# Moving the scans' first copies out of PSUM to ScalarE, and some products to other banks

## The chip, the cores and the metric

The kernel runs on one core of a Trainium2 chip. TensorE multiplies matrices and writes to PSUM, which has eight banks of 512 f32 values in each of 128 partitions; VectorE and ScalarE read PSUM and work on SBUF; GpSimd works on SBUF alone; the queues of SyncE and ScalarE issue DMAs here. The profile calls them PE (with PEld for its weight loads), DVE, ACT, POOL and SP. The metric is the device time of one run in microseconds (us), lower is better.

## The reference

A trunk of two residual layers on 512 tokens of width 1024: a spatial-gating MLP, a gated convolutional FFN, an RWKV-7 time mixing, a second FFN, and a final RMS norm, all in float32. The change lies in the time mixing, whose core for each of 16 heads of width 64 is

```python
def step(state, inp):
    r_t, w_t, k_t, v_t, a_t, b_t = inp
    sa = jnp.einsum('bhvk,bhk->bhv', state, a_t)
    state = (state * w_t[:, :, None, :]
             + sa[..., None] * b_t[:, :, None, :]
             + v_t[..., None] * k_t[:, :, None, :])
    y_t = jnp.einsum('bhvk,bhk->bhv', state, r_t)
    return state, y_t
...
bonus = jnp.sum(r_h * k_h * r_k.astype(f32), -1, keepdims=True) * v_h
y = (y + bonus.reshape(B, S, D)).astype(h.dtype)
return (y * g) @ w_o
```

with y normalized for each head before the bonus is added.

## The kernel before

Activations lie transposed: features on the 128 partitions, the 512 tokens along the free dimension, eight tiles of two heads each (a "pair"). A dense product is made of three matmuls of rounded high and low parts (lines 325 to 327, `mm3`).

The recurrence is done in chunks of 64 tokens (`NCH` = 8). For each pair, `products` (lines 970 to 988) makes the triangular matrices of all chunks, and `invert(g)` inverts them for a head group g of four pairs: a long chain of small VectorE steps (lines 1042 to 1061), then block products on TensorE (lines 1081 and 1084) with copies on ScalarE (lines 1089, 1094, 1096). `scan(g)` then goes through the eight chunks of a group in order, twice (g = 0 and 1). A chunk has three steps, with a `yield` after each:

1. TensorE makes the first products of the four pairs into the first half of a bank `us` (line 1292); VectorE copies them to `wt` in SBUF (line 1295); TensorE adds the old state's part to the output bank `e` (line 1296); GpSimd scales the state (line 1301).
2. TensorE multiplies `wt` by the inverse into the second half of `us` (line 1305): the solutions, for head 0 of each pair in partitions 0 to 63, for head 1 in 64 to 127. VectorE copies the first half of the partitions into `vu` (line 1306), ScalarE the second (line 1307).
3. TensorE makes the new state's part from `vu` (line 1312), VectorE adds it to the scaled state (line 1316, two instructions), which the next chunk's line 1292 reads; TensorE finishes the outputs in `e` (line 1317), and ScalarE copies them to `y` (line 1320).

After every second chunk, `finish` normalizes the outputs: a square (line 1333), a sum (line 1338), a scaling (line 1348), a transpose on TensorE into "aux" (line 1354), and the combination with the bonus (line 1357).

`weave` runs other work between these steps, at rates written out by hand: `fill` is a chain of `projections` (keys and values, dense products into banks "mm"), `gates` and `project` (the output projection, into "mm"); `gate_mix` makes operands (lines 1105, 1106, 237, 238). For each value, `value(m, v)` makes two products more: four centring matmuls (line 865) into a bank that ScalarE copies out in four parts (line 870), and, once the pair m is in the set `done`, the bonus product (line 880), which VectorE multiplies by v (line 882). `done` has all `KT` = 8 pairs when `pairs` has ended, a little before `scan(0)`.

PSUM has four tags, "mm", "aux", "e" and "us", with two banks each; a tile that asks for a bank waits until one of its tag is free. The first product of `scan` uses one bank of "us" and one of "e" in each chunk.

The order of the instructions on each engine is planned when the program is built: a planner with its own estimates of durations gives an engine the instruction traced earliest of those that it takes to be ready. `issue_after` puts instructions behind a given one on its engine; `step` does so for each step of `finish`, behind the last instructions traced on TensorE and VectorE. Two engines that touch the same bank are made to wait for each other. At run time each engine keeps the planned order.

Of the kernel before, what the change touches and what calls it, by code (L numbers as in the profile page):

```python
# [22 lines left out]
KT = 8  # L23
# [121 lines left out]
class Emit:  # L145
# [622 lines left out]
    def rwkv_main(self, r, ctx, gain):  # L768
        nc, tc, A = self.nc, self.tc, self.A
        V, S, G = nc.vector, nc.scalar, nc.gpsimd  # L770
        h0, h1 = slice(0, 64), slice(64, 128)
        H = (h0, h1)
# [6 lines left out]
        def tile_(shape, tag, bufs):  # L779
            return ep.tile(shape, F32, tag=tag, bufs=bufs, name=self.uid(tag))  # L780
# [7 lines left out]
        def bc(t, n):  # L788
            return t.unsqueeze(2).to_broadcast([t.shape[0], t.shape[1], n])

        ks, used, done, vdone = {}, set(), set(), set()
        l2 = []

        ti = [ip.tile([P, 4, NCH, C], F32, name=f"ti{g}") for g in range(2)]
# [13 lines left out]
        def projections():  # L808
# [29 lines left out]
            for m in range(KT):  # L838
                a = self.acc("mm")
                w = load.take()  # L840
                if m == KT - 2:
                    ga["w"] = load_gate(0)
                for n, _ in enumerate(self.dense_steps(a, w, xv)):
                    yield
                    next(late, None)
                    if m == KT - 1 and n == 0:
                        gw[0] = gate_weights(ga["w"])
                        ga["parts"] = self.gate_parts()
                    if m == KT - 1 and len(gx) < 2:
                        gx.append(gate_mix(len(gx)))  # L850
                for _ in late:
                    yield
                v = ip.tile([P, T], F32, tag="v", bufs=1, name=self.uid("v"))
                S.copy(v, a)
                late = value(m, v)
# [3 lines left out]
        def value(m, v):  # L859
            g, i = divmod(m, 4)  # L860

            vt = ip.tile([P, NCH, C], F32, tag="vt", bufs=1, name=self.uid("vt"))
            q = self.acc("mm")
            for b in range(4):
                nc.tensor.matmul(q[:, b * P:(b + 1) * P], v[:, b * P:(b + 1) * P], self.c("center", P),
                                 start=True, stop=True)
            q4 = q.rearrange("p (b h f) -> p b h f", b=4, h=2)
            for hd in range(2):
                for par in range(2):
                    S.copy(vt[H[1 - hd], par::2, :], q4[H[par], :, hd, :])  # L870
            nc.sync.dma_start(vtd[:, :, m].rearrange("c p f -> p c f"), vt)
            yield
            yield

            while m not in done:
                yield
            wb = ip.tile([P, P], F32, tag="wb", bufs=1, name=self.uid("wb"))
            S.activation(wb, self.c("bones", P), AF.Copy, scale=self.p("r_k", m))
            q = self.acc("mm")
            nc.tensor.matmul(q, wb, rt[g][:, i, :], start=True, stop=True)  # L880
            b = rt[g][:, i, :]
            V.tensor_tensor(b, q, v, ALU.mult)  # L882
            S.activation(b, b, AF.Identity, bias=self.p("ln_b", m))
            vdone.add(m)
            yield
# [372 lines left out]
        def scan(g, late=iter(())):  # L1258

            ih = [(i, hd) for i in range(4) for hd in (1, 0)]  # L1260
            y = None

            def batch(one, lead=None):

                for n, (i, hd) in enumerate(ih):
                    with ExitStack() as behind:
                        if lead is not None:
                            behind.enter_context(tc.issue_after(lead))
                        one(i, hd, n)
                    if lead is None:  # L1270
                        lead = self.last(mybir.EngineType.PE)
                return lead

            for c in range(NCH):
                last = c == NCH - 1
                if (g, c) not in chunks:
                    load(g, c)
                st, bt, vu = chunks.pop((g, c))
                if (g, c) != (1, NCH - 1):
                    load(g + last, (c + 1) % NCH)  # L1280
                if c % 2 == 0:
                    y = tile_([P, 4, 2, C], "y", 3)
                us = self.acc("us").rearrange("p (a i f) -> p a i f", a=2, i=4)
                e = self.acc("e")
                spare[:] = [e[:, 256:]]
                e = e.rearrange("p (a i f) -> p a i f", a=2, i=4)

                def both(i, hd, n):
                    o = C + P * hd + n * C
                    return st[i][:, o:o + C]  # L1290

                lead = batch(lambda i, hd, n: nc.tensor.matmul(us[H[hd], 0, i, :], both(i, hd, 0), vu[:, hd, i, :],
                                                               start=True, stop=True))
                wt = tile_([P, 4, C], "wt", 4)
                V.tensor_copy(wt, us[:, 0])
                batch(lambda i, hd, n: nc.tensor.matmul(e[H[hd], 0, i, :], st[i][H[hd], 0:C], vu[H[hd], hd, i, :],
                                                        start=i == 0, stop=False, skip_group_check=True), lead)
                if not last:
                    s0 = tile_([P, 4, C], "wt", 4)
                    for hd in range(2):  # L1300
                        G.tensor_tensor(s0[H[hd]], vu[H[hd], hd], bc(gc[H[hd], 4 * g:4 * g + 4, c], C), ALU.mult)
                self.step(late)
                yield
                for i, hd in ih:
                    nc.tensor.matmul(us[H[hd], 1, i, :], ti[g][H[hd], i, c, :], wt[H[hd], i, :], start=True, stop=True)  # L1305
                V.tensor_copy(vu[h0, 0], us[h0, 1])
                S.copy(vu[h1, 1], us[h1, 1])
                self.step(late)
                yield
                lead = None  # L1310
                if not last:
                    lead = batch(lambda i, hd, n: nc.tensor.matmul(us[H[hd], 0, i, :], bt[:, i, hd, :], vu[:, hd, i, :],
                                                                   start=True, stop=True))
                    nvu = chunks[g, c + 1][2]
                    for hd in range(2):
                        V.tensor_tensor(nvu[H[hd], hd], us[H[hd], 0], s0[H[hd]], ALU.add)
                batch(lambda i, hd, n: nc.tensor.matmul(e[H[hd], 0, i, :], both(i, hd, 1), vu[:, hd, i, :],
                                                        start=False, stop=True, skip_group_check=True), lead)
                for hd in range(2):
                    S.copy(y[H[c % 2], :, hd, :], e[H[hd], 0])  # L1320
                self.step(late)
                yield
                if c % 2 == 1:
                    yield from late
                    late = finish(g, c // 2, y)
            left.append(late)
# [102 lines left out]
        for _ in range(LEAD):  # L1429
            next(fill, None)  # L1430
        self.weave(scan(0), inv, fill, *RATES[2], ktiles=STEPS[2])
        for _ in inv:
            pass
        self.weave(scan(1, left.pop()), None, fill, *RATES[3], ktiles=STEPS[3])
        rest, left = left.pop(), None
        next(rest)
# [79 lines left out]
```

## Time and profile before

| | before |
|---|---|
| median of 3 runs (lowest to highest) | 1250.29 us (1249.78 to 1250.6) |
| the profiled execution | 1250.9 us |
| its span | 1248.8 us |
| granted TensorE clock | 0.999 |

The profile has one row for each instruction of one execution. A row of a group tells the line, engine, operation, output and inputs with their shapes and the count, then busy time, the mean ns of one, and the idle time of the engine before them with what ended it. A row of the timeline has the start and length in us first, and in brackets the idle time before it with its releaser. Matmuls overlap, so two starts are closer together than the length of one.

### The profile page before, as it was taken

Reading aid. Unit: us, or ns where it says so; the run is one execution under the profiler, and the core shown is the slowest. Engines: PE = TensorE matmul, PEld = TensorE weight load, DVE = VectorE, ACT = ScalarE, POOL = GpSimd, SP = SyncE. Lnnn points to the kernel's source line nnn. Section 1 sums busy time; section 2 is a strip of 40 time slices with the busy share of each in tenths; the row PEclk is TensorE's granted clock in tenths of the full one; section 3 lists DMA queues with packets and bytes.
Section 4 is the critical chain, followed back from the end, with each engine's and each line's share of the span. In section 5 each row is a group of like instructions: output and inputs, shape, how many; then the busy total and the mean of one; then the engine's idle time right before and its main releaser. Section 6 shows DMA issues by size and latency. Waiting matters only on the chain. (4 is left out here: it accounts for less than half of the span.)

```text
span 1248.8 us, 19409 instructions
## 1 busy us (share of the span) xinstructions
PE 1230.6 (99%) x7535; PEld 998.3 (80%) x7535; DVE 852.0 (68%) x1418; ACT 631.5 (51%) x1089; POOL 83.0 (7%) x106
## 2 busy tenths in 40 slices
PE   9999999999999999999999999999999999999997
PEld 7878888888888888877777777778888888888886
DVE  5566568888986444774989698766777777772323
ACT  6544445555554433475777657433544444442322
POOL 1100200000000010000000012322000000000000
PEclk9999999999999999999999999999999999999999
DMA  8232457877656776326878788654232233233332
GB/s 274 92 109 80 132 170 233 249 243 243 215 171 201 228 221 193 95 92 182 228 203 240 210 259 237 221 170 128 92 101 92 94 101 102 89 93 98 105 93 81
DMA packets 125132, 201.65 MB, mean 161 GB/s; under 512 B 39856, under 2 KB 63152, under 8 KB 125040
## 3 DMA queue, kind: packets, MB, share of 16 engines
q10 hardware_dynamic: 38976, 112.87, 29.6%
q1 hardware_dynamic: 86064, 87.54, 22.7%
q8 instruction: 59, 0.97, 0.3%
q14 instruction: 33, 0.27, 0.1%
HBM read 152.93 MB, written 47.45 MB: 160 GB/s over the span
## 5 line engine op out<-in xcount | busy, mean ns | idle before, releaser
L237 ACT CAST w<-w 128x512 fp32r<-128x512 f32 x340 | 205.9, 611 | 344.2 <-PE aux L327 89.1
L238 DVE TENSOR_TENSOR w<-w,w 128x512 fp32r<-128x512 f32 x340 | 230.2, 679 | 180.3 <-ACT w L237 179.8
L325 PE MATMUL mm<-mxh,w 128*128 128x512 f32 x408 | 168.2, 412 | 2.1 <-DVE rt L882 1.6
L327 PE MATMUL mm<-mxh,w 128*128 128x512 f32 x408 | 160.2, 393 | 0.0
L326 PE MATMUL mm<-mxl,w 128*128 128x512 f32 x408 | 160.0, 392 | 0.0
L325 PEld LDWEIGHTS mm<-mxh,w 128*128 128x128 f32 x408 | 76.7, 188 | 23.8 <-issue 4.4
L327 PEld LDWEIGHTS mm<-mxh,w 128*128 128x128 f32 x408 | 76.6, 188 | 16.6 <-issue 0.4
L326 PEld LDWEIGHTS mm<-mxl,w 128*128 128x128 f32 x408 | 76.7, 188 | 15.8 <-issue 1.7
L575 ACT ACTIVATE cv<-z,par 128x512 f32<-128x512 f32 x88 | 71.7, 817 | 34.9 <-DVE z L573 30.1
L325 PE MATMUL aux<-mxh,w 128*128 128x512 f32 x216 | 84.5, 391 | 0.0
L325 PE MATMUL us<-mxh,w 128*128 128x512 f32 x216 | 84.5, 391 | 0.0
L327 PE MATMUL aux<-mxh,w 128*128 128x512 f32 x216 | 84.2, 390 | 0.0
L326 PE MATMUL us<-mxl,w 128*128 128x512 f32 x216 | 84.1, 389 | 0.0
L326 PE MATMUL aux<-mxl,w 128*128 128x512 f32 x216 | 84.1, 389 | 0.0
L327 PE MATMUL us<-mxh,w 128*128 128x512 f32 x216 | 84.1, 389 | 0.0
L354 POOL TENSOR_TENSOR ss<-ss,sq 128x512 f32<-128x512 f32 x24 | 31.8, 1327 | 761.0 <-ACT sq L352 761.0
L325 PE MATMUL e<-mxh,w 128*128 128x512 f32 x208 | 81.4, 392 | 0.0
L326 PE MATMUL e<-mxl,w 128*128 128x512 f32 x208 | 81.2, 390 | 0.0
L327 PE MATMUL e<-mxh,w 128*128 128x512 f32 x208 | 81.0, 389 | 0.0
L576 DVE SCALAR_TENSOR_TENSOR cv<-z,par,cv 128x512 f32<-128x512 f32 x88 | 66.0, 751 | 19.4 <-ACT cv L575 19.4
L577 DVE SCALAR_TENSOR_TENSOR cv<-z,par,cv 128x512 f32<-128x512 f32 x88 | 66.0, 752 | 2.9
L238 DVE TENSOR_TENSOR pwl<-pw,pwh 128x512 fp32r<-128x512 f32 (+1 forms) x51 | 34.8, 682 | 21.1 <-DMA wod<-pwl 7.2
(1107 smaller groups left out, 2564.6 us busy)
## 6 DMA issues: line engine op xcount, KB each, us to landing
w<-in_wup ACTq DMA_DIRECT2D x88, 512.0 KB, 3.7
w<-in_wdn ACTq DMA_DIRECT2D x32, 512.0 KB, 3.6
st<-std SPq DMA_DIRECT2D x15, 640.0 KB, 6.3
w<-wkd ACTq DMA_DIRECT2D x16, 512.0 KB, 5.0
w<-wvd ACTq DMA_DIRECT2D x16, 512.0 KB, 4.9
w<-wod ACTq DMA_DIRECT2D x16, 512.0 KB, 4.4
w<-in_wdn ACTq DMA_DIRECT2D x16, 384.0 KB, 3.5
w<-in_wsu ACTq DMA_DIRECT2D x8, 512.0 KB, 3.7
```

What stands on the lines that cost most here:

```text
L237: nc.scalar.copy(hi[r, :n], src)
L238: (lo_eng or nc.vector).tensor_tensor(lo[r, :n], src, hi[r, :n].bitcast(F32), ALU.subtract)
L325: mm(acc, wh, xh, start=first, stop=False)
L326: mm(acc, wh, xl, start=False, stop=False)
L327: mm(acc, wl, xh, start=False, stop=last)
L354: nc.gpsimd.tensor_tensor(self.ss, self.ss, self.sq, ALU.add)
L575: nc.scalar.activation(c, z[:, 2:], AF.Identity, scale=cw(2, i), bias=self.p("conv_b", l * 44 + i))
L576: nc.vector.scalar_tensor_tensor(c, z[:, 1:T + 1], cw(1, i), c, ALU.mult, ALU.add)
L577: nc.vector.scalar_tensor_tensor(c, z[:, 0:T], cw(0, i), c, ALU.mult, ALU.add)
```

## The change

```diff
         def value(m, v):
             g, i = divmod(m, 4)
 
+            def bank():
+                return self.acc("mm" if len(done) < KT else "aux")
+
             vt = ip.tile([P, NCH, C], F32, tag="vt", bufs=1, name=self.uid("vt"))
-            q = self.acc("mm")
+            q = bank()
...
             S.activation(wb, self.c("bones", P), AF.Copy, scale=self.p("r_k", m))
-            q = self.acc("mm")
+            q = bank()
...
-                us = self.acc("us").rearrange("p (a i f) -> p a i f", a=2, i=4)
+                us, ux = (self.acc("us").rearrange("p (a i f) -> p a i f", a=2, i=4) for _ in range(2))
...
-                V.tensor_copy(wt, us[:, 0])
+                S.copy(wt, us[:, 0])
...
                 for i, hd in ih:
-                    nc.tensor.matmul(us[H[hd], 1, i, :], ti[g][H[hd], i, c, :], wt[H[hd], i, :], start=True, stop=True)
+                    nc.tensor.matmul((us, ux)[hd][H[hd], 1, i, :], ti[g][H[hd], i, c, :], wt[H[hd], i, :], start=True, stop=True)
                 V.tensor_copy(vu[h0, 0], us[h0, 1])
-                S.copy(vu[h1, 1], us[h1, 1])
+                S.copy(vu[h1, 1], ux[h1, 1])
```

In each chunk of both scans the copy of the first products (line 1295) is made by ScalarE. The solutions of head 1 go into a second bank of "us", `ux`, from which ScalarE copies them. In `value`, both products are put into a bank of "aux" in place of "mm" when they are traced after all pairs are done.

## The prediction

> **What bounds the kernel now.** I read the first part of the page, then the windows of the two scans, then the waits, and last the timeline at single places.
>
> ```profile
> span 1248.8 us, 19409 instructions
> ...
> PE 1230.6 (99%) x7535; PEld 998.3 (80%) x7535; DVE 852.0 (68%) x1418; ACT 631.5 (51%) x1089; POOL 83.0 (7%) x106
> ```
>
> TensorE is the bound: it is busy for all but 18 us of the span. A change that takes no matmul away can win only idle time of TensorE. All of this change lies in the two scans and the work woven into them, from 719 us (the last products of `products`) to 846 us. The next rows are windows of that part: length, then busy time of PE, PEld, DVE, ACT and POOL (with counts), clock, DMA share, GB/s.
>
> ```profile
> 719.00:728.50 9.50, 8.12 (x132) 5.88 (x130) 8.88 (x26) 7.13 (x16) 1.25 (x2) 1.00 0.59 162
> 728.50:767.60 39.10, 36.69 (x520) 27.12 (x519) 36.96 (x89) 22.41 (x49) 10.38 (x12) 1.00 0.94 286
> 767.60:788.50 20.90, 19.32 (x461) 15.27 (x460) 14.77 (x31) 16.65 (x28) 6.48 (x9) 1.00 0.70 214
> 788.50:846.00 57.50, 56.77 (x780) 43.30 (x780) 39.67 (x87) 20.36 (x47) 15.62 (x16) 1.00 0.55 181
> ```
>
> TensorE is idle for 1.4 + 2.4 + 1.6 + 0.7 = 6.1 us of these 127 us. That is the ceiling, about 0.5% of the kernel. From 728.5 to 767.6 VectorE is nearly full as well (36.96 of 39.10 us, with the inversion for the second head group), while ScalarE works 22.41 us. From 767.6 to 788.5 it is the other way about: ScalarE 16.65 of 20.90, VectorE 14.77. So VectorE has too much to do in the first stretch and ScalarE in the second.
>
> What ended TensorE's idle time from 719 to 846 us (total, times, longest):
>
> ```profile
> PE us L1305 <- DVE wt L1295: 2.2, 3, 0.9
> PE mm L325 <- DVE rt L882: 1.6, 2, 1.4
> PE us L1292 <- PE e L1317: 0.6, 1, 0.6
> PE e L1317 <- issue: 0.4, 1, 0.4
> PE aux L1354 <- DVE y L1348: 0.4, 1, 0.4
> PE us L1312 <- ACT vu L1307: 0.3, 1, 0.3
> PE mm L880 <- ACT vt L870: 0.3, 1, 0.3
> PE aux L1081 <- ACT off L1094: 0.2, 1, 0.2
> ```
>
> Together 6.0 us, which agrees with the windows. Four rows belong to the three edits: the wait for the copy L1295, the waits for a bank of "mm" that the values hold (readers L882 and L870), and the wait for L1307. They add up to 2.2 + 1.6 + 0.3 + 0.3 = 4.4 us. The places of the four longest:
>
> ```profile
> 727.00 0.50 PE L325 MATMUL mm<-mxh,w 128*128 128x512 f32 x1 [1.38 <-DVE rt L882]
> ...
> 730.95 0.68 PE L1305 MATMUL us<-wt,ti 64*64 64x64 f32 x16 [0.65 <-DVE wt L1295]
> ...
> 759.50 0.68 PE L1305 MATMUL us<-wt,ti 64*64 64x64 f32 x16 [0.65 <-DVE wt L1295]
> ...
> 786.17 0.68 PE L1305 MATMUL us<-wt,ti 64*64 64x64 f32 x16 [0.94 <-DVE wt L1295]
> ```
>
> **The change part by part.** *Values in "aux".* At 727.00 a new accumulator of a projection finds no bank: one of the two of "mm" is full, the other holds the bonus product until L882 has read it, and L882 stands in VectorE's queue among the inversion's steps. As I read the loops, that product (the fifth value's) is traced in the steps behind the last pairs, when all are done, so it moves to "aux", as do both products of the last three values; no instruction is added. This takes away 1.6 us and, where the second product of the last value waits for the copies of the first (L870), 0.3 us: 1.9 us. In "aux" the values meet the transposes L1354 and the inversion's products, with two banks for all. Each holds its bank for its readers only, as it does now; I put a new wait there at nothing, and at most at the 1.9 us that the same products cost in "mm".
>
> *The copy on ScalarE.* Durations (mean ns behind the bar's busy time), VectorE first, then ScalarE:
>
> ```profile
> L1295 DVE COPY wt<-us 128x256 f32<-128x256 f32 x16 | 6.8, 423 | 1.1 <-PE us L1292 0.8
> ...
> L1306 DVE COPY vu<-us 64x256 f32<-64x256 f32 x15 | 6.2, 413 | 8.4 <-PE us L1305 8.4
> ```
>
> ```profile
> L1307 ACT COPY vu<-us 64x256 f32<-64x256 f32 x15 | 5.5, 367 | 27.4 <-DVE vu L1306 24.1 <-issue 3.1
> ...
> L1204 ACT CAST mxh<-rt 128x256 fp32r<-128x256 f32 x4 | 1.4, 402 | 0.5 <-DVE rt L1200 0.5
> ```
>
> Sixteen copies of 0.42 us (6.8 us) leave VectorE. A ScalarE copy of 128x256 out of PSUM is not in the trace: the same number of columns out of PSUM takes 0.37 us (L1307), a cast of the same shape 0.40 us. I take 0.37 us; the difference would be 0.5 us of ScalarE time over 16 chunks, which nothing waits for. What counts is not these 0.05 us but the queue: at 730.95, 759.50 and 786.17 the copy stood behind other work of VectorE. If ScalarE is free when L1292 ends, all 2.2 us go. Behind the copy on ScalarE stand casts of the gates, copies of values and inversion, and the issue of weight loads:
>
> ```profile
> w<-wod ACTq DMA_DIRECT2D x16, 512.0 KB, 4.4
> ```
>
> The copy waits for a group of 16 matmuls (0.68 us in the rows of L1305), so a load can be issued that much later; the loads are ordered a weight ahead, and I cost this at nothing (at most 0.7 us, once, if a weight comes late).
>
> The Trainium skill (page "ScalarE: Activation LUTs", Rules for kernel authors) speaks against this edit: simple arithmetic belongs on VectorE, which it puts at up to about three times as fast per element in bf16. The rows here are f32 out of PSUM and show ScalarE slightly ahead, 367 against 413 ns for the same 64x256 shape. By the rule taken at its word a copy would last up to 1.3 us, 16 times, and the 2.2 us would turn into a loss; by the rows they do not, and I go by the rows.
>
> *The halves of the solutions in two banks.* L1307 follows L1306 every time, because the program makes two engines on one bank wait for each other (24.1 us of ScalarE's idle time ends there). Apart, L1307 can start with L1306, and the solutions are complete about 0.4 us earlier in each chunk. Elsewhere dense matmuls cover that; the one place where TensorE waits for L1307 gives 0.3 us. A chunk now takes both banks of "us", so the next chunk's L1292 finds one only when L1307 or L1316 has read it. It needs L1316's result anyway: nothing.
>
> *What keeps the sum from 4.4 us.* Of it, 1.9 + (2.2 - 0.9) = 3.2 us lie before 767.6, where VectorE is almost full. L1306 and L1316 stay on VectorE in a fixed order among the inversion's steps, so TensorE cannot run further ahead than VectorE does:
>
> ```profile
> 734.40 0.67 DVE L1042 STREAM_TRANSPOSE li<-li 128x256 f32<-128x256 f32 x1
> ...
> 734.96 0.37 DVE L1316 TENSOR_TENSOR vu<-us,wt 64x256 f32<-64x256 f32 x1
> ```
>
> Here, at the end of the first chunk, L1316 follows an inversion step without idle time, and the next chunk's L1292 waits for it. What VectorE gains is five copies of 0.42 us (chunks 0 to 4), 2.1 us, and at most its 39.10 - 36.96 = 2.1 us of idle time. So the 3.2 us become between 2.1 (idle time of no use) and 3.2. I take 2.2, near the lower end, since the row shows VectorE without slack at the place that decides. What is late next is then L1316. From 767.6 on the 0.9 and the 0.3 us remain; against them I set 0.2 us for copies queued on the fuller ScalarE (bounds in the last rival). Sum: 2.2 + 0.9 + 0.3 - 0.2 = **3.2 us**. After 846 us TensorE has work throughout, so this reaches the end.
>
> **The base.** The profiled run took 1250.9 us, 2.1 us more than its span of 1248.8 and 0.6 us above the median of 1250.29. 1250.9 - 3.2 = 1247.7 in that run, and the median becomes **1247.1 us**.
>
> **The rivals.** *The whole of it.* If the order planned at build time puts L1306 and L1316 ahead of inversion steps, nothing caps the gain: 4.4 us, and with all other waits 6.0 us at most: 1245.9, at the lowest 1244.3. For it: the order is planned anew. Against: the inversion's steps are traced earlier, so the planner prefers them.
>
> *VectorE's order takes it back.* TensorE reaches L1312 and L1292 earlier and waits there for L1306 and L1316. Then of the 3.2 us only one copy's time or so is kept early on, and what is saved later is half lost to ScalarE: 0.4 + 1.2 / 2 = 1.0 us, 1249.3. For it: VectorE is 94.5% busy there. Against: the inversion's end is not awaited for long, so its steps can slip.
>
> *The fifth value stays in "mm".* If its bonus product is traced one step before the last pair is counted as done, the bank is chosen as now and the 1.6 us stay. 0.3 + 1.3 us are left before 767.6, which VectorE can follow: 1.6 + 0.9 + 0.3 - 0.2 = 2.6 us at best, and some 2.2 with the cap, 1248.1. For it: the product follows close behind the last pairs' matmuls. Against: it comes with the last steps of the first inversion, which the program walks through after the pairs.
>
> *Slower: the copy gets stuck in ScalarE's queue.* It decides where an instruction that is itself waiting is planned ahead of the copy.
>
> ```profile
> 737.97 0.68 PE L1305 MATMUL us<-wt,ti 64*64 64x64 f32 x16
> ...
> 738.95 0.62 ACT L237 CAST mxh<-sq 128x512 fp32r<-128x512 f32 x1 [2.57 <-DVE sq L1106]
> ...
> 769.37 1.04 ACT L1089 COPY ti<-li 32x1024 f32<-32x1024 f32 x1
> ...
> 769.51 0.39 PE L1305 MATMUL us<-wt,ti 64*64 64x64 f32 x6
> ```
>
> Behind the cast L237 the copy would end at 738.95 + 0.62 + 0.37 = 739.94, 2.0 us after L1305 starts today. Behind the inversion's copy L1089 it would end at 770.78, 1.3 us late. Two of each are 6.6 us; the 2.2 us for the copy are then not won, the other 2.2 are: 1250.3 + 6.6 - 2.2 = 1254.7. It turns the sign beyond some 2.2 us of such waits, so from two of them on. Against it: at most chunks ScalarE is idle when L1292 ends. The Trainium skill (page "Perfetto Trace Analysis", Per-engine timelines) has ScalarE and VectorE as strict FIFO; L1307's rows, which wait while later work stands behind, agree.
>
> **How the numbers follow.** Forecast 0.40, the whole of it 0.15, taken back 0.23, fifth value unmoved 0.10, slower 0.12. A measurement of this kernel tells about 0.2%, 2.5 us, from no change. Faster by more: nearly all of the forecast (0.36), the first rival and a part of the third (0.04), 0.55; within: the rest of the forecast (0.04), of the third (0.06) and the second, 0.33; slower: 0.12, by the last. The range goes from 1244.3 (every wait gone) to 1251.0 (the second rival and the smallest cases of the last).
>
> **What would show it.** In the changed profile L1295's group is on ScalarE at about 370 ns, x16; the 24.1 us before L1307 are gone; the waits of L325 for L882 and of L1305 for VectorE are gone; TensorE's idle time from 719 to the scans' end falls from 6.0 to some 2.8 us, and a wait of L1292 or L1312 for L1316 or L1306 appears. The inversion's steps end about 2 us earlier. I am wrong if L1305 waits for ScalarE by more than 1 us in all, if the values wait in "aux", or if TensorE's idle time moves to another place of the scans.

## The result and the profile after

The changed kernel takes 1248.05 us (median of 19 runs, 1247.38 to 1250.88), the kernel before, in 19 runs beside it, 1250.39 us. The ratio is 0.9981, with a 95% interval from 0.9975 to 0.9987: 2.3 us less, where 3.2 were forecast. The profiled execution took 1249.26 us. Its page:

```profile
span 1247.5 us, 19410 instructions
...
PE 1230.1 (99%) x7535; PEld 998.0 (80%) x7535; DVE 846.3 (68%) x1402; ACT 638.1 (51%) x1105; POOL 81.9 (7%) x106
```

Sixteen instructions have left VectorE (1418 to 1402) and come to ScalarE (1089 to 1105). TensorE does the same work. The windows of the scans again; columns as before:

```profile
719.00:728.50 9.50, 9.50 (x166) 7.48 (x166) 8.86 (x27) 7.12 (x15) 0.42 (x1) 1.00 0.54 150
728.50:767.60 39.10, 35.78 (x516) 26.38 (x514) 35.78 (x85) 24.41 (x55) 10.90 (x15) 1.00 0.92 287
767.60:788.50 20.90, 20.48 (x491) 16.43 (x487) 14.13 (x29) 18.39 (x34) 6.43 (x8) 1.00 0.70 225
788.50:846.00 57.50, 56.62 (x753) 43.10 (x752) 36.33 (x78) 23.59 (x54) 15.19 (x16) 1.00 0.57 185
```

TensorE's idle time is now 0 + 3.3 + 0.4 + 0.9 = 4.6 us, against 6.1. It has gone from the first window, fallen from 1.6 to 0.4 us in the third, and *grown* in the second, from 2.4 to 3.3 us. What ended it (total, times, longest):

```profile
PE us L1315 <- DVE rb L1309: 1.4, 1, 1.4
PE us L1295 <- issue: 1.0, 2, 0.8
PE mm L1129 <- ACT mxh L237: 0.8, 1, 0.8
PE us L1315 <- DVE vu L1309: 0.7, 1, 0.7
PE us L1308 <- ACT wt L1298: 0.2, 1, 0.2
PE aux L868 <- ACT v L854: 0.2, 1, 0.2
```

The lines of the scan have numbers higher by 3 than before, so L1315 is the old L1312 (the new state), L1309 the old L1306 (VectorE's copy of the solutions), L1295 the old L1292 (the first products) and L1298 the copy that moved. The waits for a bank of "mm" are gone, and the waits of 2.2 us for the copy have become one of 0.2. In their place stand two waits for L1309, 2.1 us, that were not there. The moved copy and its neighbour on ScalarE, by groups, and what ended their idle time:

```profile
L1298 ACT COPY wt<-us 128x256 f32<-128x256 f32 x16 | 6.0, 373 | 9.1 <-PE us L1295 8.8
...
L1310 ACT COPY vu<-us 64x256 f32<-64x256 f32 x15 | 5.5, 367 | 17.4 <-PE us L1308 14.4 <-DMA st<-std 2.0 <-issue 0.9
```

A copy lasts 373 ns, and ScalarE mostly stands ready when the products end: it waits for TensorE (8.8 us) and TensorE hardly for it. L1310 waits for its own products, no longer for VectorE's copy of the other half.

**Where the gain comes and goes.** The work ahead of the scans shifts by up to some us between executions. So I measure each chunk from the last product of `products` in the same trace. The rows for that product and for the start of chunks 0, 1, 5 and 8 (the first of the second scan), before:

```profile
719.55 0.27 PE L984 MATMUL us<-dg,bk 64*128 64x64 f32 x1
...
728.59 0.33 PE L1292 MATMUL us<-rb,mxh 128*64 128x64 f32 x3
...
735.85 0.69 PE L1292 MATMUL us<-vu,st 128*64 128x64 f32 x16
...
767.66 0.28 PE L1292 MATMUL us<-vu,st 128*64 128x64 f32 x2
...
789.05 0.35 PE L1292 MATMUL us<-vu,st 128*64 128x64 f32 x6
```

and after, with the two rows of chunk 0 that lie between:

```profile
720.38 0.27 PE L987 MATMUL us<-dg,bk 64*128 64x64 f32 x1
...
727.74 0.34 PE L1295 MATMUL us<-rb,mxh 128*64 128x64 f32 x4
...
729.62 0.68 PE L1308 MATMUL us<-wt,ti 64*64 64x64 f32 x16
...
733.97 0.69 PE L1315 MATMUL us<-rb,ss 128*64 128x64 f32 x16 [1.42 <-DVE rb L1309]
...
736.84 0.69 PE L1295 MATMUL us<-vu,st 128*64 128x64 f32 x16 [0.82 <-issue]
...
767.10 0.69 PE L1295 MATMUL us<-vu,st 128*64 128x64 f32 x16
...
787.77 0.64 PE L1295 MATMUL us<-vu,st 128*64 128x64 f32 x16
```

Chunk 0 starts 728.59 - 719.55 = 9.04 us behind that product before, and 727.74 - 720.38 = 7.36 after: 1.7 us are won. Chunk 1: 16.30 and 16.46, so nothing is left of it. Chunk 5: 48.11 and 46.72, a gain of 1.4; chunk 8: 69.50 and 67.39, 2.1. The kernel's end has the same 2.1 us. (Matmuls of the gates and values move across the chunks' starts, so only the stretch up to chunk 1 and the end are read as gains.) Not all of the 2.1 us is idle time of TensorE. From that product to the end its idle time falls from 13.8 to 12.4 us, and the busy time recorded for the same 3700 matmuls from 515.45 to 514.74 us. What shortens the busy time is not shown. What takes back the 1.7 us stands in VectorE's rows of chunk 0, before and then after:

```profile
730.47 0.42 DVE L1295 COPY wt<-us 128x256 f32<-128x256 f32 x1
730.81 0.39 DVE L1060 TENSOR_TENSOR pr<-li 128x234 f32<-128x234 f32 x1
731.24 0.68 DVE L258 TENSOR_TENSOR gw<-w,gw 32x512 fp32r<-32x512 f32 x1
731.95 0.42 DVE L1306 COPY rb<-us 64x256 f32<-64x256 f32 x1
```

```profile
731.38 0.40 DVE L1063 TENSOR_TENSOR pr<-li 128x234 f32<-128x234 f32 x1
731.82 0.40 DVE L1064 TENSOR_TENSOR li<-li,pr 128x234 f32<-128x234 f32 x1
732.25 0.41 DVE L1063 TENSOR_TENSOR pr<-li 128x238 f32<-128x238 f32 x1
732.70 0.68 DVE L258 TENSOR_TENSOR gw<-w,gw 32x512 fp32r<-32x512 f32 x1
733.41 0.42 DVE L1309 COPY rb<-us 64x256 f32<-64x256 f32 x1
...
735.88 0.86 DVE L1319 TENSOR_TENSOR vu<-us,wt 64x256 f32<-64x256 f32 x2
```

The solutions are ready at 729.62 + 0.68 = 730.30, and their copy starts at 733.41, 3.1 us later: VectorE has no idle time, the copy of `wt` is gone from its queue, and the plan has put steps of the inversion (L1063, L1064) in its place. Counted from the last product, L1309 starts at 13.03 us, L1306 before at 12.40. For the 0.82 us ahead of chunk 1's L1295 the profile names no releaser ("issue"). They end 0.10 us behind L1319, which is over at 735.88 + 0.86 = 736.74, so I read them as a wait for L1319.

### The profile page after: what moved, and what is told of

Read it like the earlier page. It is cut to its first block, busy times and chain, and to the rows that moved or that the text cites. A ratio compares the mean times of both kernels' runs of the same rounds, so it can differ in the third digit from the quotient of the medians.

```text
span 1247.5 us, 19410 instructions
## 1 busy us (share of the span) xinstructions
PE 1230.1 (99%) x7535; PEld 998.0 (80%) x7535; DVE 846.3 (68%) x1402; ACT 638.1 (51%) x1105; POOL 81.9 (7%) x106
## 5 line engine op out<-in xcount | busy, mean ns | idle before, releaser
L237 ACT CAST w<-w 128x512 fp32r<-128x512 f32 x340 | 206.3, 611 | 359.8 <-PE aux L327 91.9
L238 DVE TENSOR_TENSOR w<-w,w 128x512 fp32r<-128x512 f32 x340 | 230.4, 680 | 183.3 <-ACT w L237 182.8
L325 PE MATMUL mm<-mxh,w 128*128 128x512 f32 x408 | 168.0, 412 | 0.1
L325 PEld LDWEIGHTS mm<-mxh,w 128*128 128x128 f32 x408 | 76.6, 188 | 20.8 <-issue 4.4
L325 PE MATMUL aux<-mxh,w 128*128 128x512 f32 x216 | 84.5, 391 | 0.0
L325 PE MATMUL us<-mxh,w 128*128 128x512 f32 x216 | 84.5, 391 | 0.0
L325 PE MATMUL e<-mxh,w 128*128 128x512 f32 x208 | 81.4, 391 | 0.0
L325 PEld LDWEIGHTS aux<-mxh,w 128*128 128x128 f32 x216 | 40.5, 188 | 9.0 <-issue 0.5
```

Source lines behind the costliest of these rows:

```text
L237: nc.scalar.copy(hi[r, :n], src)
L238: (lo_eng or nc.vector).tensor_tensor(lo[r, :n], src, hi[r, :n].bitcast(F32), ALU.subtract)
L325: mm(acc, wh, xh, start=first, stop=False)
```

## The experiments

**The theory**: TensorE's waits are for VectorE in its planned order, so each edit moves the wait to VectorE's next late instruction and the three gains don't add. **The rivals**: each edit has a gain of its own and they add; or it is one copy in chunk 0 alone, or VectorE's mere amount of work, that takes the gain back. In what follows a ratio is to runs of the kernel before on the same chip, with a 95% interval; "in the trace" is the end of the kernel measured from the last product of `products`, after less before, so that what lies ahead of the scans does not count.

### Each part alone, and without each part

The copy alone:

```diff
-                V.tensor_copy(wt, us[:, 0])
+                S.copy(wt, us[:, 0])
```

> Only the copy of the first products is on ScalarE; values' products and the solutions' halves stay as before. Theory of VectorE's order: TensorE's waits for that copy (2.2 us in all before) go, the waits for a bank of "mm" (1.6 us) stay; of the 1.3 us before the seventh chunk some is taken back by L1306 and L1316 on VectorE. The time falls by 1.3 to 2.0 us against before (ratio 0.9984 to 0.9990). Rival, the order planned anew: the gain of the whole change comes from where the planner happens to put the work, so a part alone may give anything between +1.5 and -2.5 us, and the waits that go are not those that the part addresses.

The values' banks alone (`bank()` for both products of `value`):

```diff
-            q = self.acc("mm")
+            q = bank()
```

> Only the values' products are in "aux" once all pairs are done. Theory of VectorE's order: the waits of L325 for L882 and of L880 for L870 go (1.9 us), but VectorE keeps all its copies, so TensorE waits for the copy or for L1306 and L1316 instead, and only 0.3 to 1.0 us of it reach the end (ratio 0.9992 to 0.9998). Rival, values' banks decide: the full 1.9 us (0.9985).

The solutions' halves alone (`ux`):

```diff
-                    nc.tensor.matmul(us[H[hd], 1, i, :], ti[g][H[hd], i, c, :], wt[H[hd], i, :], start=True, stop=True)
+                    nc.tensor.matmul((us, ux)[hd][H[hd], 1, i, :], ti[g][H[hd], i, c, :], wt[H[hd], i, :], start=True, stop=True)
```

> Only the solutions' halves are in two banks. Both theories of VectorE's order and of the waits: L1307 starts with L1306, and the one wait of TensorE for it (0.3 us) goes: 0 to 0.6 us less than before (ratio 0.9995 to 1.0). Rival, the order planned anew: more than 1 us either way.

The whole change without the values' banks:

```diff
-            q = bank()
+            q = self.acc("mm")
```

> The whole change without the values' banks: copy on ScalarE and halves in two banks. Theory of VectorE's order: the 1.7 us by which the values' banks start the first scan earlier are lost again at its second chunk, so leaving them out costs nothing: 2.0 to 2.9 us less than before (ratio 0.9977 to 0.9984), with the wait of L325 for L882 (1.4 us) back and the wait for the first chunk's L1306 gone. Rival, the parts add up: 1.2 us (what the values' banks gave alone) are missing from the whole change, 1.1 us less than before (0.9991).

The whole change without the copy:

```diff
-                S.copy(wt, us[:, 0])
+                V.tensor_copy(wt, us[:, 0])
```

> The whole change without the copy: the values' products in "aux" and the solutions' halves in two banks, while VectorE keeps the 16 copies to wt. Theory (the gain comes from the copy's place, the two bank edits are given back at the next wait for VectorE): ratio 0.9990 to 1.0000, no better than either bank edit alone; the wait of L325 for L882 is gone, the first chunk starts 1.7 us earlier, and a wait of L1308 for VectorE's wt of over 1.5 us in all takes its place. Rival (the parts add, and the copy is worth only its own 0.9 us from 767.6 us on): ratio 0.9985 or below.

What was measured. The last two columns need the section on the clock below; "others" are the executions with a mean clock of 0.998 or more, their mean time less that of such executions of the kernel before beside them (for the whole change, less its median, 1250.39).

| kernel | ratio | end, in the trace | executions with mean clock 0.997 or less | others, us |
|---|---|---|---|---|
| whole change | 0.9981 [0.9975, 0.9987] | -2.1 | 1 of 19 | -2.2 |
| copy alone | 0.9982 [0.9974, 0.9991] | -1.9 | 0 of 11 | -1.9 |
| values' banks alone | 0.9990 [0.9981, 0.9999] | -0.3 | 8 of 11 | -1.9 (3) |
| halves alone | 0.9996 [0.9987, 1.0004] | -0.4 | 0 of 11 | -0.5 |
| copy and halves | 0.9984 [0.9975, 0.9993] | -1.5 | 1 of 11 | -2.0 |
| banks and halves | 0.9989 [0.9980, 0.9998] | -1.1 | 7 of 11 | -2.5 (4) |

The copy alone gives as much as the whole change. Its 1.9 us lie within the 1.3 to 2.0 that I had expected of it, its ratio a little below the 0.9984 to 0.9990. The halves give 0.4 to 0.5 us, with an interval that includes no change; and the parts don't add: 1.9 + 0.3 + 0.4 would be 2.6 us in the trace, with the last column 1.9 + 1.9 + 0.5 = 4.3. The last kernel was to decide between "worth no more than a bank edit" (0.9990 to 1.0000) and "adds" (0.9985 or below). At 0.9989 with that interval it decides neither by its time. In the two kernels with the values' banks and without the copy, TensorE's largest wait is the same (waits from 719 to 846 us of banks and halves):

```profile
PE us L1308 <- DVE wt L1298: 2.2, 2, 2.0
```

That is the theory's picture: chunk 0 starts 1.7 us earlier and stands 2.0 us at the next instruction that needs VectorE, the copy. But it isn't the whole of what these two lost:

### The clock behind the hole

Windows of banks and halves around that wait (PEclk is the third number from the right, here 1.00 or 0.51):

```profile
727.40:730.80 3.40, 1.73 (x35) 1.33 (x34) 3.19 (x8) 3.05 (x5) 1.36 (x2) 1.00 0.49 133
730.80:732.20 1.40, 0.89 (x18) 0.82 (x19) 1.36 (x4) 0.12 (x1) 0.00 (x0) 1.00 0.94 337
732.20:735.70 3.50, 3.50 (x12) 2.52 (x11) 3.14 (x8) 1.72 (x5) 0.00 (x0) 0.51 1.02 342
```

TensorE is idle for half of 727.4 to 730.8, and from 732.2 to 735.7 its clock is granted at half; it costs some 3.5 x 0.49 = 1.7 us. VectorE feels it too: its addition in chunk 0 waits 1.05 us for the slow matmuls.

```profile
736.49 0.88 DVE L1319 TENSOR_TENSOR vu<-us,wt 64x256 f32<-64x256 f32 x2 [1.05 <-PE us L1315]
```

The trace of the values' banks alone has the same dip at the same place (PEclk 0.51 from 731.8 to 735.3). The traces of the kernel before, of the changed one, of the copy alone and of copy and halves have no dip in the scans. In the two traces that have it the mean clock of the execution is 0.997. Sorted by that, the two kernels win 1.9 and 2.5 us when the clock stays up, in few executions (3 and 4) and sorted only after the fact. Their traces say the same without sorting: less the 1.7 us of the dip, the ends would stand at some -2.0 and -2.8 us. So I read the table so: the copy's move and the banks are two ways to the same 2 us, and what the copy has over the banks is that it leaves no hole of 2 us at chunk 0.

### What holds chunk 0

The changed kernel with the gate weights' low parts (L258, L238), which stand ahead of L1309, on GpSimd:

```diff
-            self.stack(ws, w32[0:32, 512:], False)
-            return (*self.split(ep, w32[:, 0:512], [P, 512], "gw", bufs=1), ws)
+            self.stack(ws, w32[0:32, 512:], False, lo_eng=G)
+            return (*self.split(ep, w32[:, 0:512], [P, 512], "gw", bufs=1, lo_eng=G), ws)
```

> The whole change, and the two subtractions that split a gate's weights (some 1.4 us, of which the first group's stand on VectorE between the first chunk's solutions and its new state) are on GpSimd. Theory of VectorE's order: TensorE's wait of 1.4 us for the first chunk's L1309, and a part of the 0.8 us before the next chunk's first products, go: 0.8 to 1.6 us less than the whole change (ratio to before 0.9968 to 0.9975). Rival, the lost time lies elsewhere (the inversion's steps simply move up, and L1319 is as late as it was): within 0.3 us of the whole change (0.9979 to 0.9983).

It took 1.0006 [0.9997, 1.0015], in the trace +1.25 us: a miss. The wait of L1315 for L1309 grew from 1.4 to 2.9 us, for the reason in VectorE's and then GpSimd's rows of this kernel:

```profile
730.82 1.35 DVE L1063 TENSOR_TENSOR pr<-li 128x228 f32<-128x228 f32 x1
732.20 1.52 DVE L1064 TENSOR_TENSOR li<-li,pr 128x228 f32<-128x228 f32 x1
733.76 0.40 DVE L1063 TENSOR_TENSOR pr<-li 128x234 f32<-128x234 f32 x1
```

```profile
730.61 1.30 POOL L258 TENSOR_TENSOR gw<-w,gw 32x512 fp32r<-32x512 f32 x1
732.19 1.28 POOL L238 TENSOR_TENSOR gwl<-w,gwh 128x512 fp32r<-128x512 f32 x1 [0.28 <-ACT gwh L237]
```

While GpSimd runs, a VectorE step of 0.40 us takes 1.35 and 1.52 us: two steps lose 2.1 us, more than the two subtractions cost on VectorE itself (L258 and L238 in the changed kernel: 0.68 us each).

Then chunk 0's copy of the solutions on ScalarE, on top of the change:

```diff
-                V.tensor_copy(vu[h0, 0], us[h0, 1])
+                (S.copy if g == c == 0 else V.tensor_copy)(vu[h0, 0], us[h0, 1])
```

> The whole change, and in the first chunk of the first scan ScalarE copies both halves of the solutions, so L1309 of that chunk leaves VectorE. Theory that VectorE's order as a whole holds the first chunk: TensorE's wait of 1.4 us before L1315 goes, but L1319, which stands on VectorE behind the inversion's steps, is as late as before, and the next chunk's first products start no earlier: within 0.5 us of the whole change (ratio to before 0.9977 to 0.9985). Rival, L1309's place alone is the loss: 1.0 to 1.6 us less than the whole change (0.9968 to 0.9973).

In the trace -2.1 us, as the change itself: the wait for L1309 of chunk 0 is gone, and one of 2.2 us of the next chunk's L1295 has come:

```profile
737.69 0.88 DVE L1319 TENSOR_TENSOR vu<-us,wt 64x256 f32<-64x256 f32 x2
```

```profile
738.66 0.69 PE L1295 MATMUL us<-vu,st 128*64 128x64 f32 x16 [2.24 <-issue]
```

The profile names no releaser, but L1295 starts 0.09 us after L1319 is over (737.69 + 0.88 = 738.57). L1319 is as late as in the changed kernel, 15.46 us after the last product against 15.50: the plan has put one more step of the inversion ahead of it. So it isn't one copy; this part of the theory holds. The time, 0.9990 [0.9982, 0.9999], came out above what I gave; 6 of 11 executions had a mean clock of 0.997 or less, behind this hole of 2.2 us or elsewhere (the profiled one had its dip near 20 us, ahead of the scans), and the other 5 are as short as the changed kernel's.

Is it VectorE's amount of work? Two kernels leave out two of three elimination steps of the second inversion, one with the code of before, one with the change:

```diff
-                if j == 1:
+                if g == 1 and j % 3 != 1:
+                    pass
+                elif j == 1:
```

> The kernel before, with two of every three steps of the second group's inversion on VectorE left out (outputs of that group are not the reference's; the matmuls stay). VectorE then has room in the first scan. Theory of VectorE's order: most of TensorE's waits for VectorE in the first scan vanish without any of the three edits: 2 to 4 us less than before (ratio 0.997 to 0.9985). Rival, the waits come from banks and from the two engines' turns on one bank: less than 1 us.

> The whole change with the same two of three steps of the second group's inversion left out (outputs of that group are not the reference's). Theory of VectorE's order: with room on VectorE nothing takes back the values' banks' gain, and the early wait for L1309 goes; 3 to 5 us less than before the change (ratio 0.996 to 0.9976), at most 1.5 us less than the shortened kernel without the change. Rival, the order planned anew: the same 2 to 2.5 us between the two shortened kernels as between the two whole ones.

| with the inversion cut | ratio | end, in the trace |
|---|---|---|
| code of before | 0.9983 [0.9974, 0.9992] | -2.4 |
| code of after | 0.9986 [0.9977, 0.9995] | -1.0 |

With less for VectorE to do, the kernel before is as fast as the changed one, and TensorE's waits for the copy to `wt` fall from 2.2 to 0.5 us: those waits are VectorE's. But the change then gives nothing more: 0.9986 lies above the 0.9960 to 0.9976 that I gave, a miss. Chunk 0's copy comes late again, and TensorE waits 2.1 us for it (rows of VectorE, cut and changed; two lines more in this file make the old L1306 L1311):

```profile
730.46 2.05 DVE L1045 STREAM_TRANSPOSE ix<-li 128x256 f32<-128x256 f32 x4
732.37 0.60 DVE L1045 STREAM_TRANSPOSE li<-li 128x256 f32<-128x256 f32 x1
733.00 0.68 DVE L258 TENSOR_TENSOR gw<-w,gw 32x512 fp32r<-32x512 f32 x1
733.71 0.42 DVE L1311 COPY rb<-us 64x256 f32<-64x256 f32 x1
```

The steps are gone, and the plan has pulled five transposes of the inversion ahead of the copy. So less work alone doesn't bring the copy forward: the order holds chunk 0. Why the plan takes the copy to be due so late is not known from these runs.

The last test of the order: more of the inversion before the scan, and the next side step held behind VectorE's part of chunk 0.

```diff
+                    self.behind = int(g == c == 0)
...
-            self.step(ahead, (mybir.EngineType.PE,))
+            for _ in range(ahead_n.pop(0) if ahead_n else 0):
+                self.step(ahead, (mybir.EngineType.PE,))
...
-                self.step(side, (mybir.EngineType.PE,))
+                self.step(side, (mybir.EngineType.PE, mybir.EngineType.DVE)[:1 + self.behind])
+                self.behind = 0
```

(`ahead_n` is `[5, 5, 5]`.)

> The whole change, and the inversion's steps are traced so that all that follow the thirteenth or so stand on VectorE behind the first chunk's L1319; five of its steps come ahead of L1309 after the bonus product L885, in place of ten, and L1319 follows at once. Theory that VectorE's planned order takes the values' banks' 1.7 us back at the first chunk: TensorE's wait of 1.4 us before L1315 goes, the second chunk starts about 1.5 us earlier than before, and 1.0 to 2.0 us of it reach the end beyond the whole change (ratio to before 0.9965 to 0.9973). Rival, VectorE has that much to do whatever the order, so the inversion's end or a later chunk takes it back: within 0.5 us of the whole change (0.9977 to 0.9985).

It took 1.0044 [1.0027, 1.0061]: a miss. At the place that it was made for it did what the theory says: no wait for chunk 0's copy is left, and chunk 1 starts 1.0 us earlier than before instead of 0.2 us later. There TensorE now waits 1.4 us for a DMA, the load of the values into `vu`, and no longer for VectorE:

```profile
735.24 0.69 PE L1296 MATMUL us<-vu,st 128*64 128x64 f32 x16 [1.36 <-DMA vu<-vtd]
```

After that TensorE got several short holes close together, and then the clock (windows, columns as above):

```profile
758.30:761.70 3.40, 2.22 (x42) 1.39 (x40) 3.37 (x8) 2.73 (x6) 0.00 (x0) 1.00 1.00 374
761.70:768.60 6.90, 6.90 (x110) 5.84 (x108) 3.49 (x8) 5.18 (x9) 3.18 (x3) 0.51 0.53 104
768.60:775.30 6.70, 5.87 (x166) 4.24 (x164) 3.18 (x5) 5.85 (x10) 0.02 (x1) 1.00 0.62 187
775.30:785.70 10.40, 9.78 (x124) 7.68 (x124) 4.88 (x12) 6.82 (x14) 1.85 (x4) 0.51 0.31 105
```

17.3 us at half the clock cost 8.5 us, more than the 7.9 us by which this trace ends late. Without the dips the kernel would stand at some -0.6 us, still short of the change: the gain at chunk 1 isn't kept to the end, and that isn't explained by the clock.

### Where the copy pays

The kernel before with the copy on ScalarE only in chunks 4 and 7 of the first scan, where two of its three waits of 0.65 us or more stood, and with all the other copies:

```diff
-                V.tensor_copy(wt, us[:, 0])
+                (S.copy if g == 0 and c in (4, 7) else V.tensor_copy)(wt, us[:, 0])
```

> The kernel before, with only two of the sixteen copies on ScalarE: those of the fifth and the eighth chunk of the first scan, before which TensorE waited for VectorE (0.65 and 0.94 us). Theory that the copy pays where TensorE waits for it: 1.2 to 2.0 us less than before, nearly all that the sixteen copies gave alone (ratio 0.9984 to 0.9990). Rival, the relief of VectorE as a whole pays: less than 0.8 us (0.9994 or more).

```diff
-                V.tensor_copy(wt, us[:, 0])
+                (V.tensor_copy if g == 0 and c in (4, 7) else S.copy)(wt, us[:, 0])
```

> The kernel before, with the other fourteen copies on ScalarE and those of the fifth and the eighth chunk of the first scan on VectorE. Theory that the copy pays where TensorE waits for it: 0 to 0.8 us less than before (ratio 0.9994 to 1.0). Rival, the relief of VectorE as a whole pays: 1.2 us or more less (0.9990 or less).

The two gave 0.9996 [0.9987, 1.0004], in the trace -0.7 us, and 1.0002 [0.9994, 1.0011], in the trace 0.0; the expectation for the first, 0.9984 to 0.9990, missed. Together they are the copy alone, with 1.9 us. So the gain isn't 0.65 and 0.94 us fetched at two places: with the two copies alone TensorE waits elsewhere (L880 for L870 grew from 0.3 to 1.0 us). What the full move has besides: VectorE ends the second inversion earlier. Its last transpose, before, in the changed kernel, and with the fourteen other copies:

```profile
762.45 0.59 DVE L1042 STREAM_TRANSPOSE li<-li 128x256 f32<-128x256 f32 x1
```

```profile
760.20 0.63 DVE L1045 STREAM_TRANSPOSE li<-li 128x256 f32<-128x256 f32 x1
```

```profile
758.69 0.66 DVE L1042 STREAM_TRANSPOSE li<-li 128x256 f32<-128x256 f32 x1
```

From the last product that is 42.90, 39.82 and 40.04 us; it is 39.41 with the copy alone and 42.65 with the two copies. So the fourteen copies end the inversion 2.9 us earlier and win nothing by it, the two copies without that win 0.7 us, and all sixteen win 1.9. Neither is enough by itself. The order is planned anew in each of these kernels, though, and which instructions make up the 1.9 us was not followed further.

## Why the prediction was right, and where it was off

The direction was right, and the size about two thirds of the sum forecast: 2.1 us in the trace against 3.2. The 2.3 us of the medians lie within the 2.5 us that the prediction could not tell from no change, an outcome to which it gave 0.33, against 0.55 for a larger gain. The kind of gain was right for two thirds of it: 1.4 of the 2.1 us are idle time of TensorE. The rest is recorded busy time of the same matmuls, where the prediction had said that only idle time can be won. That part was not foreseen, and it is luck that the sum lies as near as it does.

- *Values in "aux"*: the fifth value's bonus product does move, L325 waits for no bank, and the 1.4 us ahead of chunk 0 (the 1.6 us hold a second wait, of 0.2 us, at 765.68) are won there: chunk 0 starts 1.7 us earlier. No wait for a bank of "aux" has come; the one of L868, 0.2 us, is for its operand.
- *The copy*: 373 ns against the 0.37 us taken. The waits of 2.2 us for it became 0.2 us for ScalarE, just the 0.2 us set against the sum. The Trainium skill's rule (page "ScalarE: Activation LUTs", Rules for kernel authors) that simple arithmetic belongs on VectorE has its figure for bf16. This copy, f32 out of PSUM, does not follow it: 373 ns on ScalarE, 423 ns on VectorE.
- *The halves*: 24.1 us of waits of ScalarE are gone; alone they gave 0.4 to 0.5 us, not clear of no change; forecast 0.3.
- *The cap, the step that was mis-sized.* The prediction kept 2.2 of the 3.2 us up to 767.6, "near the lower end, since the row shows VectorE without slack at the place that decides". The place was right, and the wait that it named came (L1315 for L1309, L1295 for L1319). Its price was too small. TensorE's idle time from the last product to chunk 5 fell only from 3.8 to 3.3 us, so 0.5 us were kept. (Chunk 5 starts 48.11 - 46.72 = 1.4 us earlier, but with two matmuls fewer ahead of it.) The bound of 2.1 took VectorE's copies and idle time as room that TensorE gets. The plan gave the room of chunk 0's copy to the inversion, whose end nothing awaits for long, and L1309 came 0.6 us *later* (13.03 against 12.40). Behind chunk 5 the forecast held: in the third window the idle time fell from 1.6 to 0.4 us, 1.2 us, forecast 1.0. So the early part came out as in the second rival, "VectorE's order takes it back" (0.4 us early on), and the late part as in the forecast.
- *The idle time* from 719 to 846 us went from 6.0 to 4.3 us by the waits, not to 2.8.
- *What it took for granted*: that the edits are terms of one sum. Each of two edits alone can give nearly the whole 2 us (the values' banks only where the clock stays up). Nor did the sum have a term for the clock.

## What to carry to other kernels

Where an engine keeps a planned order and is full, time that is freed on it goes to whatever the plan puts there next: look up which instruction takes the place, before counting the freed time as gain. Waits of the bound engine that lie one behind the other are one budget, not terms of a sum, so try each edit alone; the cheapest may give all. And when an edit joins small holes of TensorE into one of 2 us, look at the granted clock behind it.

## What the runs showed of the hardware

*The granted clock falls behind holes of TensorE, and returns in fixed portions.* Apart from the time behind the last matmuls, it fell to 0.50 in five traces: 3.5 us each in two at chunk 0 (the rows above), 6.9 and 10.4 us in the last test of the order, and 3.5 us each near 20 us in two others. These are 1, 2 and 3 portions of about 3.4 us, each of which costs 1.7 us. It doesn't come in every execution. Of the kernels whose longest hole in the scans is 1.4 us or less, leaving out the last test of the order, 12 of 178 executions had a mean clock of 0.997 or less (the kernel before: 8 of 104); of those with a hole of 1.8 us or more (e2, e4, e5, e7, e8 and e12 in the table below), 35 of 64.

| kernel | longest hole, us | such executions |
|---|---|---|
| values' banks alone (e2) | 2.0 | 8 of 11 |
| gate weights on GpSimd (e4) | 2.9 | 6 of 11 |
| chunk 0's solutions on ScalarE (e5) | 2.2 | 6 of 11 |
| inversion cut, code of before (e7) | 1.8 | 5 of 10 |
| inversion cut, code of after (e8) | 2.1 | 3 of 10 |
| banks and halves (e12) | 2.0 | 7 of 11 |

That the hole is the cause was not tried by itself, and the longest didn't bring the most: in the profiled executions, holes of 1.77 (e7), 2.12 (e8), 2.24 (e5) and 2.94 us (e4) in the scans passed without a fall. One place that no edit touches speaks for it. Near 18 us TensorE waits in 13 of the 14 traces for the same cast of a weight (L325 for L237, L238 in the last test of the order). In eleven of them it waited 0.68 to 1.56 us and the clock stayed up. In two it waited 1.92 and 1.97 us, and these are the two with the fall near 20 us. But one long hole is not needed: in the last test of the order the clock fell behind several short ones, none over 0.7 us. The Trainium skill (page "TensorE: Matmul & The Clock Gate", Part 1: The HAM clock gate) has the clock halved after an idle window and restored after a busy one, in free-running windows of 3.4 us. The length agrees. Two things differ: here TensorE was busy for a part of the 3.4 us just before the fall (1.42 of 3.40 us in banks and halves, 2.22 of 3.40 in the last test), and the clock stayed down for two windows while TensorE was busy throughout (6.90 of 6.90 us). Free-running windows would fit that only some executions show it.

*VectorE's steps get longer beside GpSimd's.* VectorE's steps of 0.40 us took 1.35 and 1.52 us beside GpSimd's subtractions of 1.30 and 1.28 us.
